# Expert stage with every other key tile spilled, and gates loaded for eight tiles at a time

## The chip, the cores and the metric

The kernel runs on one core of one Trainium2 chip. A core has five engines that run their own instruction streams in order: TensorE (PE, with its weight loads as PEld), VectorE (DVE), ScalarE (ACT), GpSimd (POOL) and SyncE (SP). SP, ACT and POOL also start DMA transfers, which are carried out by 16 DMA engines. The metric is device time of one execution in microseconds; the times shown are the median and the bounds of three executions. One further execution was profiled, and every duration below is from that one.

## The reference

Two blocks in a row, at 512 tokens of width 1024: a hybrid mixer with a gated convolutional feed-forward, and a block with latent attention, a conformer convolution and a PEER layer. The change touches only the last, the PEER layer, a retrieval of 16 experts per head and token out of 16,384 single-neuron experts (128 x 128 product keys):

```python
q = (xc @ w_pq).reshape(P_CHUNK, P_HEADS, 2, P_DK // 2)
s = jnp.einsum('thpd,hpkd->thpk', q, sub_keys)
s_top, i_top = lax.top_k(s, P_TOPK)
cand = s_top[..., 0, :, None] + s_top[..., 1, None, :]
best, ci = lax.top_k(cand.reshape(P_CHUNK, P_HEADS, P_TOPK * P_TOPK), P_TOPK)
expert = e1 * N_KEYS + e2
gate = jax.nn.softmax(best.astype(jnp.float32), axis=-1).astype(xc.dtype)
act = jax.nn.gelu(jnp.einsum('thkd,td->thk', u_tab[expert], xc), approximate=False)
return jnp.einsum('thk,thkd->td', gate * act, v_tab[expert])
```

## The kernel before

For the first 384 tokens (`ND`) the kernel computes the PEER layer densely. It goes over 128 *key tiles* j; tile j holds the 128 experts whose second key is j. For each tile it needs

- the activations `s` = gelu(u[j] . h) for 128 experts x 384 tokens: 8 contraction steps of 3 matmuls (each operand is split into a high and a low part), so 24 matmuls of 128x384 into one PSUM bank `psU`; below this is U of the tile;
- the gates `gg` of the same shape (zero where a token did not choose the expert), which the routing stage has written to `g_dram`;
- the product s*gg, split on ACT and DVE into `wh` and `wl`;
- the value rows `w_v[j]` (512 KB), split into `vh` and `vl`;
- 3 token blocks x 3 products x 2 halves = 18 matmuls of 128x512 into `psV`; below this is V of the tile. `psV` accumulates over all 128 tiles.

The last 128 tokens (`NG`) are done sparsely: GpSimd gathers one expert row per token (`indirect_dma_start`, 512 KB in all, into 4 buffers, `RB`), and DVE does one multiply-and-reduce (for `u_rows`) or multiply-add (for `v_rows`) of 128x1024 per gather. There are 256 of these gather steps; `gstep` spreads them over both stages.

The layer has two stages. In the *routing stage* DVE is busy with top-k and one-hot gates, and TensorE has time over; `fill` uses it to compute U of 64 tiles (`NSPILL`) ahead, and ACT writes each `s` (192 KB) to `s_dram`: these are the spilled tiles, j = 0 to 63. In the *last stage* `weights(n)` prepares the n-th tile: it loads gates when a new group of `GJ` = 4 tiles begins, gets `s` either back from `s_dram` (spilled, one DMA) or from `ucol` (load `w_u`, split it, U, gelu), multiplies by the gates, splits, loads and splits the value rows, and lets `rate` run gather steps in proportion (weight 1 for a tile whose U is computed here, 0.5 (`WS`) for a spilled one). `values(n - 4)` (`LAG` = 4) then issues V of the tile four places back. `finish` adds the residual, normalises and stores.

The order of tiles is by groups of four: four computed here (64 to 67), four spilled (0 to 3), four computed, and so on. Tiles below are numbered by their place n in this order.

All engines run in order, and a scheduler in the tile framework fixes the order at build time; the buffers decide who waits for whom: `gg` 2, `s` 3, `wraw` (raw `w_u`) 3, `whi`/`wlo` 2, `vraw` 3, `wh`/`wl` 6, `vh`/`vl` 5. All loads of the last stage but the gathers are issued by SP, in one order. A load waits on SP until its buffer is free, and what stands behind it on SP waits as well. On DVE the low part `wlo` of a tile's `w_u` (line 113) must be done before the third matmul of that tile's U (line 156).

Of the kernel before, what the change touches and what calls it, by code (L numbers as in the profile page):

```python
# [18 lines left out]
P = 128  # L19
# [27 lines left out]
WS = 0.5  # L47
# [23 lines left out]
class Kern:  # L71
# [1267 lines left out]
    def peer(self, x, rs):  # L1339
        nc, a, tc = self.nc, self.a, self.tc  # L1340
        NSP = self.nsp
        g_out = self.const("g_out", "final_g")
        gd = nc.dram_tensor("g_dram", [ND // TB, P, P, TB], F32, kind="Internal").ap()
        sd = nc.dram_tensor("s_dram", [NSP, P, ND], F32, kind="Internal").ap()
# [9 lines left out]
        pa = stack.enter_context(tc.tile_pool(name="pa", bufs=1))  # L1354
# [2 lines left out]
        h2l = self.t(self.gp, [P, KT, NT], F32R, "Z")[:, :, :SEQ]  # L1357
        self.norm_out(pa, x, rs, self.a2, h2h, h2l, bias=self.mod[:, 24:32])

        def ucol(pool, j):  # L1360
            w = self.load_w(a["w2_u"][j], lo_eng="pool" if j < NSP else "dve")
            pt = self.pt("U")[:, :ND]
            self.lin([(pt, dn)], w, h2h, h2l)
            s = snew(pool)
            nc.scalar.activation(s, pt, AF.Gelu)
            return s

        def snew(pool):
            return self.t(pool, [P, ND], F32, "s", bufs=2 if pool is pa else SB)

        todo = list(range(NSP))

        def fill(n):
            for _ in range(n):
                if todo:
                    j = todo.pop(0)
                    nc.scalar.dma_start(sd[j], ucol(pa, j))
        xg = self.t(pa, [P, TB * P], F32, "gs", bufs=3)[:, :D].rearrange("p (a b) -> p a b", a=KT)
        nc.vector.tensor_tensor(xg, f(h2h[:, :, ND:SEQ]), f(h2l[:, :, ND:SEQ]), op=ALU.add)
        xs = self.t(pa, [P, TB * P], F32, "gs", bufs=3).rearrange("p (a b) -> p a b", b=D)  # L1380
# [9 lines left out]
        st = [0.0, 0]  # L1390

        def gstep(n):
            for _ in range(n):
                next(gq, None)
                st[1] += 1
        self.route(pa, h2h, h2l, gd, fill, idx, gw, gstep)
        fill(NSP)
        stack.close()

        stack = ExitStack()  # L1400
        pb = stack.enter_context(tc.tile_pool(name="pb", bufs=1))
        self.psum(stack, "pse", U=(1, 2), V=(2, NB))
        GJ = 4
        ins, sp = list(range(NSP, P, GJ)), list(range(0, NSP, GJ))
        order = []
        while ins or sp:
            order.append((ins if ins and len(ins) * NSP >= len(sp) * (P - NSP) else sp).pop(0))
        order = [(j0, j0 + i) for j0 in order for i in range(GJ)]
        left, total = 2 * NG - st[1], NSP * WS + (P - NSP) - LEAD - TRAIL
        st[1] = 0  # L1410

        def rate(j):
            st[0] += WS if j < NSP else 1
            while st[1] * total < left * (st[0] - LEAD):
                gstep(1)
        gg = None
# [1 line left out]

        def weights(n):
            nonlocal gg  # L1420
            j0, j = order[n]
            if j == j0:
                gg = self.t(pb, [P, ND // TB, GJ, TB], F32, "gg", bufs=2)
                nc.sync.dma_start(gg, gd[:, :, j0:j0 + GJ].rearrange("a i j t -> i a j t"))
            if j < NSP:
                s = snew(pb)
                nc.sync.dma_start(s, sd[j])
            else:
                s = ucol(pb, j)
            s3 = s.rearrange("p (a b) -> p a b", b=TB)  # L1430
            nc.vector.tensor_tensor(s3, s3, gg[:, :, j - j0], op=ALU.mult)  # L1431
            wh = self.t(pb, [P, ND], F32R, "wh", bufs=LAG + 2)
            wl = self.t(pb, [P, ND], F32R, "wl", bufs=LAG + 2)
            self.split(s, wh, wl)
            raw = self.t(pb, [P, 1024], F32, "vraw", bufs=3)
            nc.sync.dma_start(raw, a["w2_v"][j])
            vh = self.t(pb, [P, 1024], F32R, "vh", bufs=LAG + 1)
            vl = self.t(pb, [P, 1024], F32R, "vl", bufs=LAG + 1)
            self.split(raw, vh, vl)
            rate(j)  # L1440
            return wh, wl, vh, vl
# [10 lines left out]
        for n in range(P + LAG):  # L1452
            if n < P:
                made[n] = weights(n)
            if LAG <= n < P:
                m = n - LAG
                for b in range(NB):
                    values(m, made[m], b)
                del made[m]
# [208 lines left out]
```

## Time and profile before

| | |
|---|---|
| median of three executions | 2794.11 us (2793.41 to 2795.52) |
| the profiled execution | 2797.2 us, span of its instructions 2795.4 us |
| mean granted TensorE clock over the span | 0.968 of full |
| PE busy | 2605.2 us (93%) |
| DVE busy | 2095.3 us (75%) |
| ACT busy | 1191.2 us (43%) |
| POOL busy | 647.2 us (23%) |
| moved by DMA | 509.98 MB |
| gate loads in the last stage | 32 of 768 KB |
| loads of spilled `s` | 64 of 192 KB |

A row of the view of stretches gives, for a piece of the span, each engine's busy time with its instructions, the granted clock, the share of the 16 DMA engines that was busy, and GB/s. A row of the order of time gives start, duration, engine, line, operation, what is written and read, and in square brackets the idle time ahead of it with what ended that. The last stage runs from about 1974 us (first U of a tile that is not spilled) to 2784 us (last matmul).

### The profile page before, as it was taken

How to read it: one execution, taken by the hardware profiler on the slowest of the kernel's cores; microseconds unless marked ns; L12 is line 12 of the kernel's file. 1: busy time of each engine (PE TensorE's matmuls, PEld its weight loads, DVE VectorE, ACT ScalarE, POOL GpSimd, SP SyncE). 2: the span in 40 equal slices, each digit the busy share in tenths (PEclk: the TensorE clock that was granted, in tenths of full speed). 3: DMA queues.
4: the chain of work that ended last, by engine and by line, in shares of the span. 5: the costliest groups of instructions: out<-in, count | busy, mean ns of one | idle time of the engine just before them, and what ended most of it. 6: DMA issues, size and time to landing. Idle time of an engine off the chain costs nothing. (4 is left out here: it accounts for less than half of the span.)

```text
span 2795.4 us, 38357 instructions
## 1 busy us (share of the span) xinstructions
PE 2605.2 (93%) x14307; PEld 2261.8 (81%) x14307; DVE 2095.3 (75%) x3679; ACT 1191.2 (43%) x1833; POOL 647.2 (23%) x456
## 2 busy tenths in 40 slices
PE   7999999999988998989998889888899999999998
PEld 6787888887877877877887888777798888888887
DVE  7546577774469999985557777999587878878875
ACT  4345443333334666765342222566333333333332
POOL 0001101110000000000015555554243444344430
PEclk9899999999998999988999999999999999999999
DMA  3110246664331111114433333687999999999993
GB/s 124 63 57 14 76 163 218 217 217 137 92 130 46 57 60 58 45 51 134 142 118 113 123 115 119 225 295 268 319 348 340 345 334 334 333 331 344 337 323 131
DMA packets 218659, 509.98 MB, mean 182 GB/s; under 512 B 23916, under 2 KB 97048, under 8 KB 218344
## 3 DMA queue, kind: packets, MB, share of 16 engines
q1 hardware_dynamic: 168344, 352.23, 36.9%
q0 software_dynamic: 37568, 136.42, 13.6%
q10 hardware_dynamic: 12560, 18.88, 1.9%
q8 instruction: 112, 1.84, 0.3%
q14 instruction: 75, 0.61, 0.1%
HBM read 457.12 MB, written 50.33 MB: 182 GB/s over the span
## 5 line engine op out<-in xcount | busy, mean ns | idle before, releaser
L118 ACT ACTIVATE whi<-wraw 128x1024 fp32r<-128x1024 f32 (+2 forms) x315 | 324.3, 1030 | 608.0 <-PE psU L154 141.6
L113 DVE TENSOR_TENSOR wlo<-wraw,whi 128x1024 fp32r<-128x1024 f32 (+2 forms) x237 | 278.4, 1175 | 157.7 <-ACT whi L118 156.9
L156 PE MATMUL psU<-X,wlo 128*128 128x384 f32 (+1 forms) x1032 | 356.8, 346 | 17.9 <-DVE wlo L113 13.4
L152 PE MATMUL psU<-X,whi 128*128 128x384 f32 (+1 forms) x1032 | 355.8, 345 | 10.3 <-ACT whi L118 8.9
L154 PE MATMUL psU<-Z,whi 128*128 128x384 f32 (+1 forms) x1032 | 354.4, 343 | 0.0
L118 ACT ACTIVATE wh<-s 128x384 fp32r<-128x384 f32 x128 | 66.8, 526 | 443.3 <-DVE s L1431 437.7
L1449 PE MATMUL psV<-vl,wh 128*128 128x512 f32 x768 | 236.6, 389 | 0.0
L1449 PE MATMUL psV<-vh,wh 128*128 128x512 f32 x768 | 236.4, 389 | 0.0
L1449 PE MATMUL psV<-vh,wl 128*128 128x512 f32 x768 | 236.4, 389 | 0.0
L1172 POOL DMA_INDIRECT row<-v_rows,rsf x128 | 179.3, 1401 | 240.9 <-DVE Y L1191 209.7
L111 POOL TENSOR_TENSOR wlo<-wraw,whi 128x1024 fp32r<-128x1024 f32 x78 | 199.6, 2561 | 137.8 <-ACT whi L118 133.6
L1172 POOL DMA_INDIRECT row<-u_rows,rsf x128 | 166.8, 1303 | 269.6 <-DVE Y L1184 233.0
L156 PEld LDWEIGHTS psU<-X,wlo 128*128 128x128 f32 x1032 | 197.5, 191 | 22.8 <-DVE wlo L113 15.9
L152 PEld LDWEIGHTS psU<-X,whi 128*128 128x128 f32 x1032 | 196.7, 191 | 18.3 <-ACT whi L118 12.4
L154 PEld LDWEIGHTS psU<-Z,whi 128*128 128x128 f32 x1032 | 196.7, 191 | 2.8
L1191 DVE SCALAR_TENSOR_TENSOR Y<-row,ckr,Y 128x1024 f32<-128x1024 f32 x128 | 164.1, 1282 | 28.4 <-DMA row<-v_rows,rsf 26.9
L872 DVE SCALAR_TENSOR_TENSOR Y<-y,cw,Y 128x512 f32<-128x512 f32 x240 | 176.1, 741 | 1.0
L1184 DVE SCALAR_TENSOR_TENSOR Y<-row,Y 128x1024 f32<-128x1024 f32 x128 | 158.3, 1237 | 21.4 <-DMA row<-u_rows,rsf 20.5
L1449 PEld LDWEIGHTS psV<-vh,wl 128*128 128x128 f32 x768 | 144.1, 188 | 29.9
L1449 PEld LDWEIGHTS psV<-vl,wh 128*128 128x128 f32 x768 | 144.1, 188 | 29.9
L113 DVE TENSOR_TENSOR vl<-vraw,vh 128x1024 fp32r<-128x1024 f32 x128 | 156.3, 1221 | 13.7 <-ACT vh L118 13.7
L1449 PEld LDWEIGHTS psV<-vh,wh 128*128 128x128 f32 x768 | 143.5, 188 | 25.2
(568 smaller groups left out, 6230.4 us busy)
## 6 DMA issues: line engine op xcount, KB each, us to landing
wraw<-w_u SPq DMA_DIRECT2D x128, 512.0 KB
vraw<-w_v SPq DMA_DIRECT2D x128, 512.0 KB
wraw<-w_mod SPq DMA_DIRECT2D x64, 512.0 KB
g_dram<-gs SPq DMA_DIRECT2D x96, 256.0 KB
gg<-g_dram SPq DMA_DIRECT2D x32, 768.0 KB
wraw<-w_up SPq DMA_DIRECT2D x44, 512.0 KB
s_dram<-s ACTq DMA_DIRECT2D x64, 192.0 KB
s<-s_dram SPq DMA_DIRECT2D x64, 192.0 KB
```

The lines of the kernel that those rows point to most:

```text
L111: self.nc.gpsimd.tensor_tensor(dst, x, f(hi), op=ALU.subtract)
L113: self.nc.vector.tensor_tensor(dst, x, f(hi), op=ALU.subtract)
L118: nc.scalar.activation(hi, src, AF.Copy)
L152: nc.tensor.matmul(o, wh, xh[:, c], start=first, stop=False)
L154: nc.tensor.matmul(o, wh, xl[:, c], start=False, stop=False)
L156: nc.tensor.matmul(o, wl, xh[:, c], start=False, stop=last)
L872: nc.vector.scalar_tensor_tensor(zc, y[:, j:j + SEQ], cw[:, ct, j:j + 1], zc, op0=ALU.mult, op1=ALU.add)
L1172: nc.gpsimd.indirect_dma_start(out=r, out_offset=None, in_=a[name], in_offset=bass.IndirectOffsetOnAxis(ap=idx[:, k:k + 1], axis=0))
L1184: self.tc.keep_in_program_order(nc.vector.scalar_tensor_tensor(scr, r, 1.0, xt, op0=ALU.mult, op1=ALU.mult, accum_out=sc[:, k:k + 1]))
L1191: self.tc.keep_in_program_order(nc.vector.scalar_tensor_tensor(vacc, r, sc[:, k:k + 1], vacc, op0=ALU.mult, op1=ALU.add))
L1449: nc.tensor.matmul(psv[b][:, h], w[:, c], v[:, h * 512:h * 512 + 512], start=first and w is wh and v is vh, stop=last and w is wl)
```

## The change

Spilled are now the odd tiles j = 1, 3, ..., 127, and the last stage takes the tiles in the order 0 to 127, so computed and spilled tiles alternate. `slot` maps a spilled tile to its place in `s_dram`. `GJ` is 8: one gate load of 1.5 MB for eight tiles, in runs of 8 x 32 x 4 = 1024 bytes, in place of two of 768 KB in runs of 512 bytes; with two buffers the gates take twice the room. The amount of matmuls, loads of `w_u`, `w_v` and `s`, and gather steps is the same; there are 16 DMA issues fewer.

```diff
+        slot = {j: (j * NSP) // P for j in range(P) if (j + 1) * NSP // P > j * NSP // P}
+
         def ucol(pool, j):
-            w = self.load_w(a["w2_u"][j], lo_eng="pool" if j < NSP else "dve")
+            w = self.load_w(a["w2_u"][j], lo_eng="pool" if j in slot else "dve")
...
-        todo = list(range(NSP))
+        todo = sorted(slot)
...
-                    nc.scalar.dma_start(sd[j], ucol(pa, j))
+                    nc.scalar.dma_start(sd[slot[j]], ucol(pa, j))
...
-        GJ = 4
-        ins, sp = list(range(NSP, P, GJ)), list(range(0, NSP, GJ))
-        order = []
-        while ins or sp:
-            order.append((ins if ins and len(ins) * NSP >= len(sp) * (P - NSP) else sp).pop(0))
-        order = [(j0, j0 + i) for j0 in order for i in range(GJ)]
+        GJ = 8
...
         def rate(j):
-            st[0] += WS if j < NSP else 1
+            st[0] += WS if j in slot else 1
...
-            j0, j = order[n]
+            j, j0 = n, n - n % GJ
             if j == j0:
                 gg = self.t(pb, [P, ND // TB, GJ, TB], F32, "gg", bufs=2)
                 nc.sync.dma_start(gg, gd[:, :, j0:j0 + GJ].rearrange("a i j t -> i a j t"))
-            if j < NSP:
+            if j in slot:
                 s = snew(pb)
-                nc.sync.dma_start(s, sd[j])
+                nc.sync.dma_start(s, sd[slot[j]])
```

Three places in the built order carry the argument. Up to the start of the last stage the orders are the same but for line numbers and names.

**First, SP early in the last stage.** Before: `gg_18529` is the third gate load (places 8 to 11), `s_18458` and `s_18495` the spilled activations of places 6 and 7, `vraw_18502`, `_18569` and `_18640` the values of places 7, 8 and 9, `gg_18809` the fourth gate load.

```order
L1424 DMA gg_18529<-g_dram 128x12x128
L1427 DMA s_18458<-s_dram 128x384
L145 DMA wraw_18670<-w_u 128x1024
L1427 DMA s_18495<-s_dram 128x384
L1436 DMA vraw_18502<-w_v 128x1024
L1436 DMA vraw_18569<-w_v 128x1024
L1436 DMA vraw_18640<-w_v 128x1024
L1424 DMA gg_18809<-g_dram 128x12x128
```

Now, at the like place on SP: `vraw_18500`, `_18567` and `_18607` are the values of places 7, 8 and 9, the three `wraw` the `w_u` of places 10, 12 and 14, `gg_18949` the third gate load (places 16 to 23), `s_18600` the spilled activations of place 9.

```order
L1433 DMA vraw_18500<-w_v 128x1024
L145 DMA wraw_18634<-w_u 128x1024
L145 DMA wraw_18739<-w_u 128x1024
L145 DMA wraw_18844<-w_u 128x1024
L1433 DMA vraw_18567<-w_v 128x1024
L1433 DMA vraw_18607<-w_v 128x1024
L1421 DMA gg_18949<-g_dram 128x12x256
L1424 DMA s_18600<-s_dram 128x384
L1433 DMA vraw_18672<-w_v 128x1024
```

The third gate load has moved ahead of a spilled `s` that is wanted soon (place 9), and it takes the buffer of the first, which is free once DVE has multiplied place 7.

**Second, DVE at the first tile whose U comes after a V that follows a spilled tile.** Before: the multiply of place 7, a gather step, its `wl` and `vl`, a gather step, then `wlo_18533`, the low part for U of place 8.

```order
L1431 TENSOR_TENSOR s_18495<-s_18495,gg_18388 128x384
L1184 SCALAR_TENSOR_TENSOR Y_12928,ckr_12828<-row_18471,Y_12928 128x1024
L113 TENSOR_TENSOR wl_18499<-s_18495,wh_18498 128x384
L113 TENSOR_TENSOR vl_18505<-vraw_18502,vh_18504 128x1024
L1184 SCALAR_TENSOR_TENSOR Y_12928,ckr_12828<-row_18474,Y_12928 128x1024
L113 TENSOR_TENSOR wlo_18533<-wraw_18531,whi_18532 128x1024
```

Now: the multiply of place 9 (`s_18600`), and `wlo_18636` for U of place 10.

```order
L1428 TENSOR_TENSOR s_18600<-s_18600,gg_18527 128x384
L1184 SCALAR_TENSOR_TENSOR Y_12928,ckr_12828<-row_18573,Y_12928 128x1024
L113 TENSOR_TENSOR wl_18604<-s_18600,wh_18603 128x384
L1184 SCALAR_TENSOR_TENSOR Y_12928,ckr_12828<-row_18576,Y_12928 128x1024
L113 TENSOR_TENSOR vl_18610<-vraw_18607,vh_18609 128x1024
L1184 SCALAR_TENSOR_TENSOR Y_12928,ckr_12828<-row_18579,Y_12928 128x1024
L113 TENSOR_TENSOR wlo_18636<-wraw_18634,whi_18635 128x1024
```

From the first gate multiply of the stage to the end of this low part DVE now has 48 instructions (10 multiplies, 10 `wl`, 10 `vl`, 3 `wlo`, 15 gather steps); before it was 37 (8, 8, 8, 2, 11).

**Third, DVE in the steady part of the last stage.** Before, at the end of the spilled group of places 28 to 31: the multiply of place 31 (`s_19764`), the rest of places 30 to 32, then `wlo_19941` for U of place 34, the third computed tile of its group. The multiplies of places 28, 29 and 30 stand ahead of this piece.

```order
L1431 TENSOR_TENSOR s_19764<-s_19764,gg_19657 128x384
L113 TENSOR_TENSOR vl_19737<-vraw_19734,vh_19736 128x1024
L1184 SCALAR_TENSOR_TENSOR Y_12928,ckr_12828<-row_19706,Y_12928 128x1024
L113 TENSOR_TENSOR wl_19768<-s_19764,wh_19767 128x384
L1184 SCALAR_TENSOR_TENSOR Y_12928,ckr_12828<-row_19740,Y_12928 128x1024
L113 TENSOR_TENSOR vl_19774<-vraw_19771,vh_19773 128x1024
L1184 SCALAR_TENSOR_TENSOR Y_12928,ckr_12828<-row_19743,Y_12928 128x1024
L113 TENSOR_TENSOR vl_19841<-vraw_19838,vh_19840 128x1024
L1184 SCALAR_TENSOR_TENSOR Y_12928,ckr_12828<-row_19777,Y_12928 128x1024
L1184 SCALAR_TENSOR_TENSOR Y_12928,ckr_12828<-row_19844,Y_12928 128x1024
L113 TENSOR_TENSOR wlo_19941<-wraw_19939,whi_19940 128x1024
```

Now: the multiply of place 29 (`s_19651`, spilled), `vl` and `wl` of it, the values of place 30, three gather steps, the multiply of place 30 (`s_19716`, computed), and directly behind it `wlo_19899` for U of place 34.

```order
L1428 TENSOR_TENSOR s_19651<-s_19651,gg_19368 128x384
L113 TENSOR_TENSOR vl_19661<-vraw_19658,vh_19660 128x1024
L113 TENSOR_TENSOR wl_19655<-s_19651,wh_19654 128x384
L1184 SCALAR_TENSOR_TENSOR Y_12928,ckr_12828<-row_19630,Y_12928 128x1024
L113 TENSOR_TENSOR vl_19726<-vraw_19723,vh_19725 128x1024
L1184 SCALAR_TENSOR_TENSOR Y_12928,ckr_12828<-row_19664,Y_12928 128x1024
L1184 SCALAR_TENSOR_TENSOR Y_12928,ckr_12828<-row_19729,Y_12928 128x1024
L1184 SCALAR_TENSOR_TENSOR Y_12928,ckr_12828<-row_19732,Y_12928 128x1024
L1428 TENSOR_TENSOR s_19716<-s_19716,gg_19368 128x384
L113 TENSOR_TENSOR wlo_19899<-wraw_19897,whi_19898 128x1024
```

The low part for place 34 stood behind four spilled activations in a row; now one spilled activation lies between two low parts, and the low part stands four places ahead of its U. On PE the order was U, V, U, V, U, V, U, V and four more V in every eight places; it is now U, V, V throughout, with U of place n+4 ahead of V of place n.

## Rows read from the trace of the kernel before

**Rows 1.** Stretches of 50 us: bounds, length, busy times, clock, DMA share, GB/s

```profile
2000.00:2050.00 50.00, 41.52 (x198) 37.23 (x197) 41.57 (x61) 14.92 (x20) 21.56 (x17) 0.90 0.94 355
2050.00:2100.00 50.00, 50.00 (x244) 44.31 (x243) 38.59 (x57) 17.43 (x24) 19.95 (x16) 1.00 0.94 329
2550.00:2600.00 50.00, 48.32 (x235) 42.67 (x234) 39.80 (x43) 15.76 (x24) 19.83 (x16) 1.00 0.92 325
```

**Rows 2.** Who waited for whom, PE, 1974 to 2786: total, times, longest

```profile
PE psU L156 <- DVE wlo L113: 13.4, 6, 8.5
```

**Rows 3.** PE in order of time, matmuls with idle time ahead of them

```profile
1988.46 0.44 PE L156 MATMUL psU<-X,wlo 128*128 128x384 f32 x1 [0.92 <-DVE wlo L113]
2024.22 0.69 PE L156 MATMUL psU<-X,wlo 128*128 128x384 f32 x1 [8.48 <-DVE wlo L113]
2433.83 0.44 PE L156 MATMUL psU<-X,wlo 128*128 128x384 f32 x1 [1.21 <-DVE wlo L113]
2586.43 0.45 PE L156 MATMUL psU<-X,wlo 128*128 128x384 f32 x1 [1.68 <-DVE wlo L113]
```

**Rows 4.** ACT in order of time, the load that came last

```profile
2015.46 1.06 ACT L118 ACTIVATE vh<-vraw 128x1024 fp32r<-128x1024 f32 x1 [6.18 <-DMA vraw<-w_v]
```

**Rows 5.** DVE in order of time, start of the stage and the late low part

```profile
1983.48 0.56 DVE L1431 TENSOR_TENSOR s<-s,gg 128x384 f32<-128x384 f32 x1 [2.68 <-DMA vraw<-w_v]
...
1993.14 1.22 DVE L113 TENSOR_TENSOR vl<-vraw,vh 128x1024 fp32r<-128x1024 f32 x1
1994.28 1.22 DVE L1184 SCALAR_TENSOR_TENSOR Y<-row,Y 128x1024 f32<-128x1024 f32 x1
...
1995.43 0.55 DVE L1431 TENSOR_TENSOR s<-s,gg 128x384 f32<-128x384 f32 x1
1995.90 1.22 DVE L1184 SCALAR_TENSOR_TENSOR Y<-row,Y 128x1024 f32<-128x1024 f32 x1
...
2022.94 1.22 DVE L113 TENSOR_TENSOR wlo<-wraw,whi 128x1024 fp32r<-128x1024 f32 x1
```

**Rows 6.** Stretches of 4 us around the long wait, columns as in rows 1

```profile
2016.00:2020.00 4.00, 0.00 (x0) 0.00 (x0) 3.04 (x5) 2.82 (x5) 1.01 (x1) 0.71 0.30 123
2020.00:2024.00 4.00, 0.00 (x0) 0.00 (x0) 4.00 (x7) 0.64 (x1) 1.72 (x2) 0.50 0.81 243
2024.00:2028.00 4.00, 3.78 (x12) 3.79 (x13) 4.00 (x6) 0.00 (x0) 2.27 (x2) 0.51 1.03 398
```

**Rows 7.** Who waited for whom, DVE, 2030 to 2786: total, times, longest

```profile
DVE s L1431 <- DMA s<-s_dram: 68.0, 26, 5.7
```

**Rows 8.** PE in order of time, two U matmuls and the V behind them

```profile
2008.72 0.33 PE L152 MATMUL psU<-X,whi 128*128 128x384 f32 x1
...
2009.07 0.62 PE L1449 MATMUL psV<-vh,wh 128*128 128x512 f32 x2
2009.53 0.62 PE L1449 MATMUL psV<-vl,wh 128*128 128x512 f32 x2
```

**Rows 9.** DMA, 2030 to 2034 (value rows and gathers): packets, MB, share

```profile
DMA packets 450, 1.65 MB, mean 412 GB/s; under 512 B 48, under 2 KB 48, under 8 KB 450
...
q1 hardware_dynamic: 280, 1.02, 63.5%
q0 software_dynamic: 170, 0.63, 39.1%
```

**Rows 10.** DMA, 1978 to 1980: SP's queue, gates alone

```profile
q1 hardware_dynamic: 854, 0.44, 86.1%
```

**Rows 11.** DMA, 945 to 948: one load of 128 runs of 1024 bytes

```profile
q1 hardware_dynamic: 144, 0.13, 14.5%
```

**Rows 12.** DMA, 1974 to 1976: ACT's queue, one spilled s stored

```profile
q10 hardware_dynamic: 144, 0.20, 26.8%
```

**Rows 13.** DMA, 1976 to 2030: share of SP's queue and of the gathers

```profile
q1 hardware_dynamic: 8960, 11.88, 65.0%
q0 software_dynamic: 1544, 5.66, 27.3%
```

## The prediction

> **What bounds the kernel now.** I read the stretches first, then PE's waits, then DVE, ACT and the DMA queues around the waits found. In the last stage PE is the bound: a stretch such as 2050 to 2100 has it busy for all of its 50 us with 244 matmuls, while DVE is at 39 us and the DMA engines at 0.94 [rows 1]. The change leaves the matmuls as they are, so it can only win what PE loses in the stage, which is little. PE waits six times, 13.4 us in all, each time for the low part of a tile's `w_u` [rows 2]: 0.92 us at 1988, 8.48 us up to 2024.2, and four waits between 2433 and 2587 [rows 3], of which the first and the last stand there, together 13.4 - 0.92 - 8.48 = 4.0 us. Their distance, (2586.43 - 2433.83) / 3 = 50.9 us, is that of eight tiles: two U matmuls take 0.35 us and two V matmuls 0.46 us [rows 8], so a U takes 4.2 us, a V 4.1 us, and eight tiles 4 x 4.2 + 8 x 4.1 = 49.6 us.
>
> The long wait is a chain of in-order engines. ACT stood 6.18 us for a load of value rows [rows 4]; DVE, behind it, reached the low part of place 8 at 2022.94 [rows 5], and PE went on at 2024.2. [...] What PE loses now is thus 0.9 + 8.5 + 1.9 = 11.3 us at the start of the stage and 4.0 us late in it.
>
> **Prices of the transfers.** All per 16 DMA engines. In 2030 to 2034 the 402 large packets took (63.5% + 39.1%) x 4 us x 16, so 163 ns each [rows 9]; 512 KB (value rows, `w_u`, one gather) is 128 of them, 1.3 us. A 512-byte gate packet took 86.1% x 2 us x 16 / 854 = 32.3 ns [rows 10]. A 1024-byte packet of a gate does not occur before; the nearest row is a small load of 128 such packets, at most 14.5% x 3 us x 16 / 128 = 54 ns [rows 11]. The bounds are 32.3 ns (as dear as now per packet) and 64.6 ns (as dear per byte); I take 54. One gate load of eight tiles is 1,536 packets, 5.2 us, against 2 x 3.1 = 6.2 us for two of four. A spilled `s` is 128 packets of 1536 bytes: 26.8% x 2 us x 16 / 128 = 67 ns [rows 12], 0.54 us.
>
> **The late waits: -4.0 us.** A spilled tile needs value rows 1.3, `s` 0.54 and half the gather rate: with 232 steps left for a weight of 89 that is 1.3 gathers, 1.7 us. Four of them with a gate load make 4 x 3.5 + 3.1 = 17.3 us of DMA, while PE works 4 x 4.1 = 16.4 us: the feed is too slow there. Four computed tiles need 4 x (2 x 1.3 + 2.6 x 1.3) + 3.1 = 27.0 against 33.2 us. DVE duly waits for spilled activations, 26 times for 68.0 us [rows 7], and a low part that stands behind four of them in DVE's order (third place) is late by then. Alternating, each pair needs 6.0 + 3.5 + 5.2 / 4 = 10.8 us against 12.4 us of PE, everywhere. And a low part stands behind one spilled activation, with V, V, U, V, V (20.6 us) still ahead of its U when it is done. I cost the late waits at nothing afterwards. What covers them is that lead; without it, up to the 4.0 us stay, or grow (rivals).
>
> **The start of the stage: +0.8 us.** First, the first gate load takes 2.1 us longer, so the first multiply moves from 1983.48 [rows 5] to 1985.6. On DVE one more low part and two more multiplies now stand ahead of `vl` of place 0; with 0.47 us for a small operation (1995.43 to 1995.90) and 1.15 us for a large one (1993.14 to 1994.28, and on to 1995.43) [rows 5] it ends at 1985.6 + 4 x 0.47 + 1.15 + 1.22 = 1989.8. PE used to have four U to cover this; now it has three, and they end where the fourth began, 1988.46 - 0.92 - 0.35 = 1987.2 [rows 3]. After two V matmuls it waits 2.2 us, in place of 0.92.
>
> Second, the long wait moves from place 8 to place 10. PE gets there after V V U V V U V V, two U matmuls, V and two V matmuls, counted from 1989.3: 2027.2. DVE needs 20 x 0.47 + 28 x 1.15 = 41.6 us of its own for the 48 instructions up to that low part: from 1985.6, also 2027.2. So without any wait of DVE the stall is 0: the lower bound. Before, the like sum was 16 x 0.47 + 21 x 1.15 = 31.7 us from 1983.48, to 2015.2, and DVE ended at 2024.2: 9.0 us of waits, all of it PE's stall. Scaled to 41.6 us that is 11.8 us: the upper bound. In between lies what DMA must bring before `s` of place 9, which now stands behind the third gate load: 3 gate loads 15.6, 10 value tiles 13.1, 5 `s` 2.7, 3 `w_u` 3.9, some 10 gathers 13.1 (12 steps stand ahead in DVE's order, 4 rows were there), and 2 us of loads still under way: 50.4 us. At the 92.3% of 1976 to 2030 [rows 13] this ends at 1976.2 + 54.6 = 2030.8, at full share at 2026.6. DVE's tail from there (2 small, 5 large operations, the last at its full 1.22) is 6.8 us, so PE goes on between 2033.4 and 2037.6, a stall of 6.2 to 10.4 us. I take 8.0, and the same 1.9 us at the lower clock. Sum: 2.2 + 8.0 + 1.9 = 12.1 against 11.3.
>
> [...]
>
> The routing stage computes 64 tiles ahead in the same order of instructions, only others; at nothing. So do the end (V of the last four places by token block, `finish`) and the 16 issues saved on SP, which waits anyway.
>
> **Sum.** -4.0 + 0.8 = -3.2 us on the profiled execution of 2797.2: 2794.0. That execution lies 3.1 us above the median of the runs, so 2791 us is predicted.
>
> **Rivals.**
> 1. *The start wait vanishes.* For it: its lower bound, and evener loads from the first tile on. Against: one wide gate load still stands ahead of `s` of place 9 and of everything behind it. Then the start costs 2.2 us and the clock does not fall: 2.2 - 11.3 - 4.0 = -13.1, 2781 us.
> 2. *The late waits stay.* For it: DVE's gathers and DMA's share of 0.92 and more also in the late stretches [rows 1] are nearly the same work. Against: the lead of 20 us. Then +0.8: 2795 us.
> 3. *Slower: the gate load holds up SP once in eight tiles.* With two buffers the load for block k+2 waits on SP until DVE has multiplied the last tile of block k; then come 5.2 us of gates, two value tiles and only then the next spilled `s`. If DVE's wait for that `s` outgrows the lead, PE stalls in each of some 14 blocks, where the late waits of now came in four. At the mean of now, 1.0 us, that is +14.0 - 4.0 + 0.8 = +10.8: 2805 us. It decides against the change from 0.23 us a block. Against it: DVE is busy for 39 of 50 us and can catch up.
>
> **How the numbers follow.** The forecast case (long wait moved, late ones gone) has 0.50 and by itself 2787 to 2795: by the stall of 6.2 to 10.4 and the packet's price. Rival 1 has 0.20, rival 2 0.17, rival 3 0.13. Some 0.2%, 5.6 us, is what a measurement can tell from no change: below 2788.5 is faster, above 2799.7 slower. Faster: 0.20 and 0.13 of the forecast case, 0.33. Slower: 0.11 of rival 3, 0.04 of rival 2 where the start goes to its upper bound (2.2 + 11.8 + 1.9 - 11.3 = +4.6, 2799), 0.15. The same: 0.52. The range reaches from 2783, within rival 1, to 2800, past rival 2's upper bound.
>
> **What would show it.** In the profile after: one PE wait of 6 to 10 us near 2027 to 2036, at a low part, with DVE ahead of it waiting for `s` from `s_dram`; a short one near 1988; none after 2100; DVE's waits for `s_dram` well below 68 us; gate packets near 54 ns. A start without a long wait makes rival 1 right; PE waits at intervals of 50 us rival 2 or 3, by their number. A change ahead of 1974 us, or another number of matmuls per 50 us in a full stretch, would make the whole argument wrong.

## The result, and the profile after

The changed kernel takes 2827.42 us, the median of four runs (2823.34 to 2831.86); the kernel before, run beside it, 2793.76 us (2792.28 to 2795.52). The ratio is 1.0125, with a 95% interval of 1.0110 to 1.0139: slower by 1.2%, outside the predicted range. The execution profiled took 2823.34 us, 26.1 us more than that of before. It is the fastest of the four, so the profiles account for 26.1 us; the medians differ by 33.7 us, and what the other 7.6 us are is not shown.

All of the 26.1 us lie in the last stage. The first U of a tile that is not spilled starts at 1973.53 us (before 1974.15), the last pair of matmuls at 2809.71 (before 2783.63). I call the distance of the two the stage's length: 836.2 us, before 809.5.

Stretches of 50 us of the changed kernel, with the columns of [rows 1]:

```profile
2000.00:2050.00 50.00, 39.35 (x180) 34.77 (x179) 35.45 (x55) 15.01 (x20) 19.98 (x16) 0.86 0.97 364
2050.00:2100.00 50.00, 50.00 (x244) 44.40 (x243) 37.00 (x54) 15.62 (x22) 19.35 (x14) 1.00 0.84 308
2550.00:2600.00 50.00, 46.06 (x213) 39.85 (x212) 39.53 (x44) 17.09 (x24) 21.68 (x16) 0.97 0.91 329
```

A full stretch has 244 matmuls in both kernels, so PE's own work is unchanged. What differs is the late stretch (213 matmuls, before 235), and the DMA share, 0.84 where it was 0.94. PE's waits in order of time (start, duration, in brackets the idle time ahead; between 2310 and 2420 five more, of 0.37, 0.43, 1.75, 0.38 and 1.55 us) answer to [rows 3]:

```profile
1988.45 1.20 PE L1446 MATMUL psV<-vh,wh 128*128 128x512 f32 x4 [1.97 <-ACT vh L118]
1990.00 1.22 PE L1446 MATMUL psV<-vl,wh 128*128 128x512 f32 x2 [0.35 <-DVE vl L113]
2039.36 0.69 PE L156 MATMUL psU<-X,wlo 128*128 128x384 f32 x1 [10.65 <-DVE wlo L113]
...
2419.05 0.45 PE L156 MATMUL psU<-X,wlo 128*128 128x384 f32 x1 [3.97 <-DVE wlo L113]
2573.92 0.69 PE L156 MATMUL psU<-X,wlo 128*128 128x384 f32 x1 [3.94 <-issue]
2677.01 0.44 PE L156 MATMUL psU<-X,wlo 128*128 128x384 f32 x1 [2.42 <-DVE wlo L113]
2730.74 0.69 PE L156 MATMUL psU<-X,wlo 128*128 128x384 f32 x1 [3.87 <-issue]
```

Nothing for 270 us after the start, then nine waits up to 2731. "Issue" says only that the profile names no releaser: DVE ended the low parts for the U of 2573.92 and of 2730.74 less than 0.1 us ahead of them, so these are waits for the low part as well. The reason is on DVE. Who waited for whom, 2030 to 2812 (total, times, longest), in place of the 68.0 us of [rows 7]:

```profile
DVE s L1428 <- DMA s<-s_dram: 148.7, 47, 10.2
```

and its long waits in order of time, two of thirteen:

```profile
2195.53 0.56 DVE L1428 TENSOR_TENSOR s<-s,gg 128x384 f32<-128x384 f32 x1 [8.01 <-DMA s<-s_dram]
2248.33 0.56 DVE L1428 TENSOR_TENSOR s<-s,gg 128x384 f32<-128x384 f32 x1 [8.14 <-DMA s<-s_dram]
```

Once in eight tiles DVE stands 5.5 to 10.2 us for one spilled activation. What stands ahead of that load shows in SP's order of time around the second of these waits:

```profile
2227.20 0.33 SPq L145 DMA_DIRECT2D wraw<-w_u  x1
2230.58 0.38 SPq L1421 DMA_DIRECT2D gg<-g_dram  x1
2231.71 3.08 SPq L1433 DMA_DIRECT2D vraw<-w_v  x2
2234.84 0.48 SPq L1424 DMA_DIRECT2D s<-s_dram  x1
2239.80 0.33 SPq L145 DMA_DIRECT2D wraw<-w_u  x1
2250.05 3.08 SPq L1433 DMA_DIRECT2D vraw<-w_v  x2
```

The gate load went out at 2230.58, and the spilled activation behind it, issued at 2234.84, let DVE go on at 2248.33, 13.5 us later. The DMA engines from 2230 to 2246 (packets, MB, share), and the stretches of 4 us after that (columns as above):

```profile
q1 hardware_dynamic: 2198, 3.65, 64.2%
q0 software_dynamic: 680, 2.47, 38.7%
```

```profile
2242.00:2246.00 4.00, 4.00 (x19) 3.34 (x18) 0.00 (x0) 0.00 (x0) 0.00 (x0) 1.00 1.04 408
2246.00:2250.00 4.00, 4.00 (x22) 3.73 (x22) 1.67 (x3) 1.07 (x2) 0.00 (x0) 1.00 0.43 170
2250.00:2254.00 4.00, 4.00 (x22) 3.61 (x21) 3.96 (x8) 1.73 (x3) 1.68 (x1) 1.00 0.45 142
```

SP's queue (q1) had 64% of the engines and the gathers (q0) 39%. Then the loop closes: while DVE stood, no buffer for value rows came free, SP issued nothing from 2239.80 to 2250.05, and the DMA engines ran at 0.43 and 0.45. PE stays busy in all of this (4.00 of 4.00): it lives on the lead of finished V operands. The gate loads follow each other at 2073.66, 2126.19, ... 2701.73, thirteen of them, so eight tiles take 52.3 us of which PE needs 49.6; some 2.7 us of lead goes in each block, and after five blocks PE begins to wait. The lead itself can be read, from the end of a low part on DVE to the matmul that needs it:

```profile
2081.12 1.22 DVE L113 TENSOR_TENSOR wlo<-wraw,whi 128x1024 fp32r<-128x1024 f32 x1
2099.12 0.34 PE L156 MATMUL psU<-X,wlo 128*128 128x384 f32 x1
...
2308.95 1.22 DVE L113 TENSOR_TENSOR wlo<-wraw,whi 128x1024 fp32r<-128x1024 f32 x1
2310.23 0.44 PE L156 MATMUL psU<-X,wlo 128*128 128x384 f32 x1 [0.37 <-issue]
```

At 2099 it is 16.8 us; the best of the next blocks are 13.3, 12.3, 8.2 and 6.0 us, and at 2310 it is 0.1.

### The profile page after: what moved, and what is told of

The parts are those of the page before. It is cut to its first block, busy times and chain, and to the rows that moved or that the text cites. A ratio compares the mean times of both kernels' runs of the same rounds, so it can differ in the third digit from the quotient of the medians.

```text
span 2821.4 us, 38235 instructions
## 1 busy us (share of the span) xinstructions
PE 2609.2 (92%) x14307; PEld 2261.9 (80%) x14307; DVE 2096.0 (74%) x3679; ACT 1188.0 (42%) x1833; POOL 666.5 (24%) x456
## 5 line engine op out<-in xcount | busy, mean ns | idle before, releaser
L1172 POOL DMA_INDIRECT row<-v_rows,rsf x128 | 189.9, 1484 | 240.4 <-DVE Y L1191 210.0
L1172 POOL DMA_INDIRECT row<-u_rows,rsf x128 | 175.9, 1374 | 279.0 <-DVE Y L1184 246.0
L152 PEld LDWEIGHTS psU<-X,whi 128*128 128x128 f32 x1032 | 197.9, 192 | 18.5 <-ACT whi L118 12.3
L1428 DVE TENSOR_TENSOR s<-s,gg 128x384 f32<-128x384 f32 x128 | 70.9, 555 | 158.8 <-DMA s<-s_dram 154.2
```

The costliest lines, as they stand in the source:

```text
L152: nc.tensor.matmul(o, wh, xh[:, c], start=first, stop=False)
L1172: nc.gpsimd.indirect_dma_start(out=r, out_offset=None, in_=a[name], in_offset=bass.IndirectOffsetOnAxis(ap=idx[:, k:k + 1], axis=0))
```

## Experiments

Theory A: the gate load of eight tiles stands in SP's queue ahead of a spilled activation that DVE wants next; DVE's wait grows with the load, and PE pays when the lead is gone. Rivals: B, the alternation itself makes each spilled activation late, since two loads of value rows that wait for DVE stand ahead of it; C, the total of DMA work; S, the size of one gate load alone, wherever it stands. A fourth, that the start alone makes the loss, can be read from the waits. All runs, with the stage's length, DVE's wait for `s` from 2030 to 2810 us, and PE's idle time in the stage at its start and after 2060:

| run | time, us | ratio to before (95%) | stage, us | DVE wait for s, us | PE idle, start + late, us |
|---|---|---|---|---|---|
| before | 2794.5 | 1 | 809.5 | 68.0 | 9.4 + 4.0 |
| changed | 2827.4 | 1.0125 (1.0110 to 1.0139) | 836.2 | 148.7 | 13.0 + 18.7 |
| `e1_gj4` | 2814.8 | 1.0072 (1.0045 to 1.0099) | 828.1 | 151.9 | 6.4 + 19.8 |
| `e3_block8` | 2805.6 | 1.0033 (1.0016 to 1.0050) | 817.7 | 51.0 | 11.3 + 8.0 |
| `e2_s_act` | 2786.2 | 0.9973 (0.9959 to 0.9988) | 802.6 | 69.5 | 6.5 + 0 |
| `e7_gg_act` | 2799.1 | 1.0019 (1.0004 to 1.0035) | 820.7 | 127.3 | 17.4 + 4.7 |
| `e10_two_gates` | 2786.4 | 0.9973 (0.9960 to 0.9986) | 806.1 | 27.6 | 7.3 + 0 |
| `e9_before_s_act` | 2791.1 | 0.9996 (0.9980 to 1.0012) | 806.0 | 63.4 | 9.5 + 1.7 |
| `e8_s_act_gj4` | 2794.9 | 0.9999 (0.9981 to 1.0018) | 808.7 | 94.9 | 11.7 + 0 |
| `e13_gj4_sact_sb6` | 2793.7 | 0.9995 (0.9981 to 1.0009) | 810.5 | 82.5 | 13.0 + 0 |
| `e14_gates_late` | 2816.5 | 1.0076 (1.0056 to 1.0096) | 827.8 | 145.3 | 9.6 + 13.5 |
| `e15_late_s_act` | 2790.4 | 0.9994 (0.9979 to 1.0009) | 806.7 | 74.0 | 10.2 + 0 |

Time is the median, stage and waits are of one profiled execution; the start of the stage varies from 1966 to 1976 us between executions, which is in the time and not in the stage. Each ratio is to runs of before on the same chip; the row of before has their median beside the first four runs. All edits are to the changed kernel, except in `e9_before_s_act`.

**`e1_gj4`: alternating, gates for four tiles.**

```diff
-        GJ = 8
+        GJ = 4
```

> Alternating tiles as in the changed kernel, but gates for four tiles at a time (768 KB, runs of 512 bytes): the order of the tiles alone. Theory A (a gate load stands ahead of a spilled s in SP's queue, and DVE waits for that s; the wait grows with the gate load): waits of about 5 us twice in eight tiles in place of 8 to 10 once, DVE's waits for s_dram 120 to 160 us, time 2810 to 2830. Rival S (the size of one gate load alone does it, a wait comes only when it is over some size): waits for s_dram under 60 us, time 2785 to 2795. Rival C (the DMA engines' total work bounds, wherever it is queued): more than the changed kernel, 2830 or over, since 512-byte packets cost 16 us more in all.

DVE waits about 5 us at every second pair in place of 5.5 to 10.2 at every fourth, in this row and three others 25 to 29 us apart:

```profile
2214.81 0.56 DVE L1428 TENSOR_TENSOR s<-s,gg 128x384 f32<-128x384 f32 x1 [5.18 <-DMA s<-s_dram]
```

The wait follows the gate load in place and size. The alternating order loses with either size; the larger load is the dearer (1.0125 against 1.0072). S falls (under 60 us of waits expected), and C (2830 us or more). So does the start alone: it costs 6.4 us of idle time here, and 19.8 lie later.

**`e3_block8`: four computed and four spilled in each eight, gates for eight.**

```diff
-        slot = {j: (j * NSP) // P for j in range(P) if (j + 1) * NSP // P > j * NSP // P}
+        slot = {j: j // 8 * 4 + j % 4 for j in range(P) if j % 8 >= 4}
```

> Gates for eight tiles at a time, but four computed and four spilled tiles in each eight, as before: the gate load alone. In its built order three value loads of computed tiles and more stand between a gate load and the next spilled s. Theory A: no long wait behind a gate load, DVE's waits for s_dram 50 to 80 us as before, time 2788 to 2800. Rival S: 2815 to 2830, with a wait of 8 us or more in each eight tiles. Rival C: 2780 to 2792, a little below before, for the cheaper packets.

In groups of four the same large gate load costs less: the next spilled activation on SP goes out 32.6 us behind it,

```profile
2221.67 0.37 SPq L1421 DMA_DIRECT2D gg<-g_dram  x1
...
2254.25 0.90 SPq L1424 DMA_DIRECT2D s<-s_dram  x2
```

and DVE's wait for `s` is 51.0 us. S, which expected 2815 us or more, and C (2780 to 2792) fall. It costs something all the same (1.0033, 2805.6 us where A allowed 2800): PE's idle time grows by 1.9 us at the start and by 4.0 late. So neither part of the change helps by itself.

**`e2_s_act`: ACT issues the spilled activations.**

```diff
-                nc.sync.dma_start(s, sd[slot[j]])
+                nc.scalar.dma_start(s, sd[slot[j]])
```

> The changed kernel with the loads of spilled s issued by ACT in place of SP: same transfers, but s no longer stands behind the gates and the value rows in SP's queue. Theory A: DVE's waits for s_dram fall from 149 to under 30 us, no PE wait after 2100, time 2780 to 2795, with the wait of some 8 to 10 us at the start of the stage still there or shorter. Rival C: the waits go elsewhere (value rows, gathers), time stays at 2820 to 2830.

This one edit takes back all and more, with the DMA work unchanged: C falls. PE's only waits in the stage, and one `s` in the orders of SP, ACT and DVE:

```profile
1984.50 2.60 PE L1446 MATMUL psV<-vh,wh 128*128 128x512 f32 x6 [2.83 <-ACT vh L118]
2027.91 0.44 PE L156 MATMUL psU<-X,wlo 128*128 128x384 f32 x1 [3.70 <-DVE wlo L113]
```

```profile
2209.31 0.38 SPq L1421 DMA_DIRECT2D gg<-g_dram  x1
2214.96 0.33 ACTq L1424 DMA_DIRECT2D s<-s_dram  x1
2222.97 0.56 DVE L1428 TENSOR_TENSOR s<-s,gg 128x384 f32<-128x384 f32 x1 [4.05 <-DMA s<-s_dram]
```

The activation is there 8.0 us after its issue, 13.7 us after the gate load; in the changed kernel 13.5 and 17.8. DVE's wait is halved (4.05 against 8.14), not gone: I had expected under 30 us in total and 69.5 were measured; whether the rest is the load's own time among the others or its late issue by ACT was not separated. But what is left PE's lead covers: from 2062 to the end of the stage the low parts are 12.6 to 18.6 us ahead of their U, in every block alike. As it beats both kernels, this is the version to keep.

**`e7_gg_act`: ACT issues the gates in place of SP.**

```diff
-                nc.sync.dma_start(gg, gd[:, :, j0:j0 + GJ].rearrange("a i j t -> i a j t"))
+                nc.scalar.dma_start(gg, gd[:, :, j0:j0 + GJ].rearrange("a i j t -> i a j t"))
```

> The changed kernel with the gate loads issued by ACT: the gates leave SP's queue, s stays in it behind two value loads. Theory A: the long waits (8 to 10 us once in eight tiles) go, those of about 1 us in each pair stay, DVE's waits for s_dram 30 to 60 us, time 2785 to 2800, unless ACT, which now waits for a free gate buffer, holds up its own work. Rival B (s is late because it stands behind value loads that wait for DVE, in each pair, gates or not): waits stay over 100 us, time 2815 to 2830. Rival C: 2820 to 2830.

The late waits of PE nearly go, but DVE's stay at 127.3 us. So A as I had put it, with the place on SP as the whole cause, is too narrow: on another queue the gates still share the engines (from 2060 to 2700 ACT's queue, with the gates, had 9.8% of them, SP's 38.9% and the gathers 43.8%, and a gate load took 18.5 us in the median to land, 12.3 in `e2_s_act`), and the spilled activation still has two value tiles ahead of it on SP (B's part); the run does not tell these two apart. The start grows to 17.4 us: DVE waits 7.45 us for the first gates (at 1984.90), in a stage that began 7 us earlier than that of the changed kernel, and PE 10.83 us ahead of its first V.

**`e10_two_gates`: the gates without their transfers.**

```diff
-            if j == j0:
+            if j == j0 and j < 2 * GJ:
```

> The changed kernel, with the gates loaded for the first sixteen tiles alone; the later tiles are multiplied by the gates of places 8 to 15. It leaves out 14 of the 16 gate loads, and nothing else. Theory A (a spilled activation waits behind the gate load in SP's order and for the DMA engines that the load fills): the waits of 8 to 10 us once in eight tiles are gone, DVE's wait for spilled activations from 2030 to 2810 us falls from 148.7 us to 20 to 60 us, PE has no wait over 1 us after 2060, and the time is 2785 to 2797 us. Theory B (with computed and spilled tiles in turn, each spilled activation stands behind two loads of value rows that wait for DVE, with or without gates): 100 us or more of that wait stay, late PE waits stay, 2805 to 2825 us. Under both the long wait near 2030 can shrink, but not by gates alone, since the first two loads are still there.

DVE's wait falls to 27.6 us and PE has no late wait. B alone would have kept 100 us. The gate loads, 14 of them, thus cost the changed kernel 836.2 - 806.1 = 30 us of the stage, more than its whole loss of 26.7.

**`e9_before_s_act`: the kernel before, ACT issues the spilled activations.**

```diff
-                nc.sync.dma_start(s, sd[j])
+                nc.scalar.dma_start(s, sd[j])
```

> The kernel before, with one edit: ACT issues the loads of spilled activations in place of SP. It tells whether the gain of the changed kernel with this edit (ratio 0.9973) is of the queue alone or needs computed and spilled tiles in turn. Theory A (queue and order together): in groups of four spilled tiles the feed of 17.3 us of DMA against 16.4 us of PE stays too slow whoever issues it, so the late waits stay at about 4 us, and the start wait at place 8 stays at 6 to 9 us: 2788 to 2797 us. Rival Q (the queue alone): the start wait falls to 2 to 4 us and the late waits go, as in the changed kernel with this edit: 2780 to 2788 us.

No change in time within the interval; the start wait stays (9.52 us at 2026.26). So the queue alone is likely not the gain of `e2_s_act`, whose start wait is 3.70 us; the two intervals (0.9980 to 1.0012 and 0.9959 to 0.9988) touch, so it isn't settled. A's detail was wrong in one thing: three of the four late waits went (one of 1.71 us is left) with the same amount of DMA work, so the sum of the feed in groups of four does not explain them.

**`e8_s_act_gj4` and `e13_gj4_sact_sb6`: smaller gate loads with ACT's queue, the second with six buffers for `s`.** Edits: those of `e1_gj4` and `e2_s_act` together; for the second also

```diff
-SB = 3
+SB = 6
```

> Computed and spilled tiles in turn, gates loaded for four tiles at a time (packets of 512 bytes), and ACT issues the loads of spilled activations. Theory A: with the spilled activation out of SP's order, the size of the gate load hardly matters any more; DVE's wait for spilled activations is 40 to 90 us, no late PE wait over 1.5 us, and the time within 0.3% of that with gates for eight tiles: 2778 to 2795 us. Rival G (what counts is the DMA time of gates, 6.2 us in two loads against 5.2 us in one for each eight tiles): 1 us more in each of 14 blocks, DVE's wait over 100 us, and 2796 to 2802 us.

> As the run with gates for four tiles and spilled activations issued by ACT, but with six buffers for activations in place of three (the room comes from the smaller gate buffers). Theory A (what is left of the wait is the load's own time behind what fills the DMA engines): loads that start two tiles earlier take it away; DVE's wait for spilled activations falls under 30 us; PE waits twice at the start alone, 2776 to 2788 us. Rival O (ACT reaches the issue no earlier, since the order on ACT and not the buffer holds it): the wait stays at 40 to 90 us and the time within 0.2% of the run with three buffers.

No late wait in either, as A has it; of the sums of DVE's waits, 94.9 us lie between the theories and 82.5 are rival O's, and more buffers change nothing in the time (rival O). What these two have more than `e2_s_act` is the start (11.7 and 13.0 us of idle time against 6.5); I put it to the third gate load, which with gates for four tiles place 8 needs. The intervals around 0.9973 and 0.9999 overlap, so that gates for eight tiles are the better choice is likely and not settled.

**`e14_gates_late` and `e15_late_s_act`: the gate load moved, on SP and with ACT's queue for `s`.**

```diff
             nc.vector.tensor_tensor(s3, s3, gg[:, :, j - j0], op=ALU.mult)
+            if j - j0 == 2 and j0 + GJ < P:
+                gn = self.t(pb, [P, ND // TB, GJ, TB], F32, "gg", bufs=2)
+                nc.vector.tensor_copy(gn[:, 0, 0, :1], s[:, :1])
+                nc.sync.dma_start(gn, gd[:, :, j0 + GJ:j0 + 2 * GJ].rearrange("a i j t -> i a j t"))
```

> The changed kernel with every gate load but the first issued after the multiply of the third tile of the eight before it (a copy of one column into the new buffer ties it there), still on SP. In SP's order it then stands right behind the w_u load that follows a spilled activation, with two loads of value rows and the next spilled activation behind it. Theory A, refined (what counts is how long the gate load's packets have run when the next spilled activation is issued; in the changed kernel that is 4.3 us): by the times of the run without gates the gate load starts 8 to 9 us ahead of the next spilled activation, so DVE's wait once in eight tiles falls from 8 to 10 us to 2 to 5, its sum from 2030 to 2810 us from 148.7 to 50 to 100 us, no late PE wait over 2 us, and 2786 to 2800 us. Rival P (any gate load between two spilled activations on SP costs the same): waits of 8 us stay, 2810 to 2830 us. At the start the third gate load moves behind the multiply of place 10: the long wait there shrinks below 6 us under A.

> The same tie of the gate loads, and ACT issues the loads of spilled activations. Theory A, refined: both remedies act on the same wait, so little is added to the run with the second alone (ratio 0.9973); DVE's wait for spilled activations 30 to 70 us, no late PE wait, a start wait of 2 to 6 us: 2778 to 2790 us. Rival T (the tie itself costs: DVE does sixteen more small operations and the gate load may come late for its first multiply): a new wait of DVE for gates at the first tile of each eight, 2790 to 2805 us.

My refinement failed and rival P holds, though the test was weaker than meant. In `e14_gates_late` the gate load goes out 7.0 and 5.4 us ahead of the spilled activation in two blocks, in place of 4.3 (8 to 9 were expected), and DVE waits 7.38 and 10.16 us behind them, as long as ever. The second block in SP's order:

```profile
2247.12 0.43 SPq L1434 DMA_DIRECT2D gg<-g_dram  x1
2249.24 3.17 SPq L1439 DMA_DIRECT2D vraw<-w_v  x2
2252.47 0.46 SPq L1426 DMA_DIRECT2D s<-s_dram  x1
```

and in DVE's:

```profile
2267.87 0.56 DVE L1430 TENSOR_TENSOR s<-s,gg 128x384 f32<-128x384 f32 x1 [10.16 <-DMA s<-s_dram]
```

From 2244 to 2268 the gathers had nearly as much of the engines as SP's whole queue:

```profile
q1 hardware_dynamic: 2451, 4.16, 49.6%
q0 software_dynamic: 1149, 4.18, 46.2%
```

So a head start of a few microseconds doesn't take DVE's wait away; I read it as before, that whatever stands between two spilled activations on SP has to pass at SP's share of the engines. The run is still less slow than the changed kernel (1.0076 against 1.0125, intervals apart): its stage is 8.4 us shorter, with 3.4 us less idle time at the start and 5.2 less later. With ACT's queue (`e15_late_s_act`) the tie neither helps nor costs much; rival T's wait for gates does not appear, but the start wait stays at 10.2 us where 2 to 6 were expected.

## Why the prediction was wrong

**What held.** PE is the bound with the same matmuls; nothing moved ahead of the stage; the mechanism at the start is as told: two short waits of 1.97 and 0.35 us for the first V (predicted 2.2, though for `vl` alone and behind two V matmuls; the longer one stood ahead of V, for `vh` on ACT), then a long one at the low part of place 10, with DVE waiting for `s` of place 9 behind the third gate load. PE got there at 2039.36 - 10.65 = 2028.7 (predicted 2027.2). DVE in order of time:

```profile
2032.57 0.56 DVE L1428 TENSOR_TENSOR s<-s,gg 128x384 f32<-128x384 f32 x1 [5.04 <-DMA s<-s_dram]
...
2038.08 1.22 DVE L113 TENSOR_TENSOR wlo<-wraw,whi 128x1024 fp32r<-128x1024 f32 x1
```

The activation came at 2032.6 (predicted 2026.6 to 2030.8). **The size of the start was off**: 10.65 us lie just above the 6.2 to 10.4 worked out, and PE went on at 0.50 of the full clock, to which it had fallen while PE waited:

```profile
2032.00:2036.00 4.00, 0.00 (x0) 0.00 (x0) 3.44 (x7) 1.58 (x2) 1.01 (x1) 0.50 0.56 222
...
2040.00:2044.00 4.00, 4.00 (x14) 4.00 (x13) 4.00 (x7) 0.00 (x0) 1.79 (x2) 0.50 0.91 320
2044.00:2048.00 4.00, 4.00 (x20) 3.60 (x20) 1.92 (x3) 1.76 (x3) 1.68 (x1) 0.95 1.02 409
```

0.95 in the last stretch is 0.4 us at half, so this cost (2044.4 - 2039.36) / 2 = 2.5 us (predicted 1.9). The runs show the clock as a share of full alone: the 1.9 us in the sums of 11.3 and 12.1 stand on 3.78 us of PE's work at 0.51 [rows 6], halved. The working had the clock fall once; it fell after the first wait too:

```profile
1988.00:1996.00 8.00, 7.20 (x24) 5.51 (x25) 8.00 (x11) 6.33 (x10) 0.00 (x0) 0.79 0.66 213
```

which is 0.21 x 8 = 1.7 us, of which 0.1 falls into the wait of 0.35 us. Together 13.0 + 2.5 + 1.6 = 17.1 us against 12.1 predicted and 11.3 before: +5.8 in place of +0.8. A small part is the packet: with the gates alone, 1979 to 1981,

```profile
q1 hardware_dynamic: 525, 0.54, 94.6%
```

a packet of 1024 bytes took 94.6% x 2 us x 16 / 525 = 57.7 ns, where I had taken 54 from an upper bound of another load; that makes 0.4 us for the first gate load. Of the later gate loads all but one (56.5, that of 2334.17) were cheaper than my 54: by the trace's records of single packets the second and third took 51.3 and 48.8 ns a packet, and that of 2230.58 took 50.5.

**The step that failed: "the late waits: -4.0 us", costed at nothing afterwards.** The stage grew by 26.7 us, of which the start has 5.8; so the late part lost 20.9 us more, where -4.0 had been predicted. Of these 18.67 - 4.04 = 14.6 us are PE's idle time. Another 4.8 us are the lower clock after the three waits of nearly 4 us; before, it was 1.00 from 2060 to the end of the stage. One of the three stretches of 8 us:

```profile
2572.00:2580.00 8.00, 6.08 (x26) 5.97 (x27) 7.95 (x10) 4.26 (x6) 3.99 (x3) 0.79 0.95 350
```

The others, from 2418 and from 2729, have 0.79 as well: 3 x 0.21 x 8 = 5.0 us, of which some 0.2 fall into the waits. The matmuls after PE resumed took 0.52 us in place of 0.34. The last 1.5 us are not explained. Three things in that step were wrong, of which the second and the third decide.

1. *The balance of a pair.* I summed 10.8 us of DMA against 12.4 of PE. `e2_s_act`, whose PE never waits there, shows the true need:

```profile
2050.00:2300.00 250.00, 250.00 (x1215) 221.98 (x1214) 207.32 (x305) 91.98 (x122) 109.10 (x80) 1.00 0.96 347
```

0.96 x 250 us over 250 / 12.4 = 20.2 pairs is 11.9 us a pair. The slack was 0.5 us and not 1.6: by the packet records the 4096-byte packets took 178 ns there on average (176 in the changed kernel), where I had 163 from 4 us, while the gates' 1024-byte packets took 49. `e2_s_act` never waits late even so; the balance left little room, but it did not fail by itself.

2. *The wait.* I had its parts (5.2 us of gates, two value tiles, the spilled activation: 8.3 us) and did not divide by the share that SP's queue gets. With the `w_u` load of 2227.20, whose packets still stood ahead, it is 9.6 us, and 9.6 / 0.642 = 15.0 us; 17.8 were measured from the gate load's issue to the use of the activation. The share is not even: the gates had the engines all but to themselves (2234 to 2238, gathers 0.5%), then value rows and activation met the gathers that DVE had set free (2240 to 2248):

```profile
q1 hardware_dynamic: 1314, 1.40, 103.1%
...
q0 software_dynamic: 499, 1.80, 56.8%
q1 hardware_dynamic: 429, 1.20, 38.4%
```

Then I priced PE's loss at 1.0 us, the mean of the late waits of before, though the mechanism that I had just named has no reason to share their size.

3. *The cover.* The lead, 20.6 us as worked out and at best 17.5 as measured, covers one wait of 8 us, but not one in each block unless DVE wins the time back. "DVE is busy for 39 of 50 us and can catch up" left DVE's waits out: from 2050 to 2300 it is busy 190.2 us and waits 51.1 (47.0 of them for `s`, in the view that gave 148.7 for the whole stage), 241 of 250. With the short gaps between its instructions nothing is left, and its pace, 52.3 us for eight tiles, becomes that of the stage.

This is rival 3, at the place and by the mechanism given, but with a loss of (20.9 + 4.0) / 14 = 1.8 us a block in place of 1.0, and its chance of 0.13 was far too low. The sum as it now stands: +5.8 at the start, +20.9 late, -0.6 since the stage began earlier, +26.1 us, where -3.2 had been predicted.

**What stays open.** 1.5 us of the late loss, and the 7.6 us by which the medians differ more than the profiles, are not explained. Why the activation of place 9 came 1.8 us later than its upper bound was not separated. Why three of four late waits go in `e9_before_s_act`, and whether the queue alone gains nothing, was not tried further. Whether gates for eight beat gates for four once ACT issues the activations lies within the spread of the runs.

## What to carry to other kernels

A feed that is fast enough on average can still set the pace, when one large load stands in a queue ahead of a small one that an in-order engine wants next (here 1.5 MB of gates ahead of 192 KB, for which DVE stood 5.5 to 10.2 us in each eight tiles): add up everything between two loads of the urgent kind, divide by the share that this queue gets of the DMA engines (64.2% and 49.6% in the two stretches read here), and compare it with what the waiting engine has free in a period, its other waits included. A lead hides such a wait once; only free time in each period pays for it again and again (here the lead fell from 16.8 us at 2099 to 0.1 at 2310). The cheap remedy here was to issue the small, urgent load from an engine whose queue holds nothing large (0.9973); moving the large one instead (`e7_gg_act`, 1.0019) gave back less.

## What the runs showed of the hardware that was not expected

Two queues that share the same 16 DMA engines are not one line: the spilled activation of 192 KB needed 13.5 us from issue to use behind gates and value rows on SP's queue and 8.0 us on ACT's, with a gate load under way on SP's queue in both. In `e2_s_act` the queues were served side by side: of the engines from 2209 to 2225 SP's queue had 60.7%, the gathers 38.1% and ACT's queue (q10), with the one activation, 3.4%; the activation landed 8.0 us after its issue, the value rows issued on SP in that stretch 11.9 us after theirs in the median. And the gathers, 1149 packets from 2244 to 2268 in `e14_gates_late`, took 46.2% of the engines while SP's queue, with loads waiting, got 49.6%.
